# Twelve hidden blocks read back on another queue, and the products for the gates on another accumulation bank

## The chip, the cores and the metric

One core of a Trainium2 chip runs the whole kernel as one program. TensorE (PE, with PEld for its weight loads), VectorE (DVE), ScalarE (ACT), GpSimd (POOL) and SyncE (SP) each run a list of instructions in a fixed order and wait for each other through semaphores. The metric is the device time of the core in microseconds, the median of several runs.

## What is computed

The reference is one decoder layer on x of 512 tokens by 2048 channels, all in fp32. Six rows of modulation come from one vector c:

```python
mod = silu(c) @ w_ada + b_ada                      # 6 rows of 2048: sh1, sc1, g1, sh2, sc2, g2
h = rmsnorm(x, norm1_g) * (1 + sc1) + sh1
x = x + g1 * hybrid_mixer(h, ...)                  # w_in, convolution and RWKV-7 heads, w_out
h = rmsnorm(x, norm2_g) * (1 + sc2) + sh2
x = x + g2 * ((silu(h @ w_ff1) * (h @ w_ff3)) @ w_ff2)   # inner width 5632
out = rmsnorm(x, norm_f_g)
```

## The kernel before

**Products.** Each fp32 matrix is split into a high half (`hi`, a cast on ACT, L89) and a low half (`lo`, a subtraction on DVE, L90), and each product is three matmuls into one PSUM bank (`mm3`, L73): high by high, high by low, low by high. Weights come from HBM in blocks of 512 KB into tiles `ws` (four buffers) and `ws2` (six more while the first two feed-forward matrices run); their halves are `wh` and `wl` (three pairs). A unit of work is one such set of blocks; `stream` (L273) fetches two units ahead, hands their splits to ACT and DVE between matmuls, and calls a unit's `before` ahead of its first matmul. The code is written in one order; a scheduler then sets the order on each engine and queue, so that a load can stand far from where the code has it. SP's queue carries all weight loads, in its fixed order; each waits until its buffer has been read.

**w_ff1 and w_ff3.** `fast_units` (L1128) computes both products with seven instead of eight block products. It runs over 11 column blocks of 512 (c = 0 to 10); each has part 0 (four units of 12 steps, left operands `xh0` to `xh11`, `xl0` to `xl11`) and part 1 (four units of 16 steps, left operands in other tiles). A step is one `mm3`. For part 1, and the third product of part 0, DVE first takes differences of weight blocks (L1416), then the low half. The sums of a column block are turned (transposed) on PE during the next one's part 0. Of the 44 blocks of 128 hidden rows that result, the first 12 are split and written to DRAM as `hidd` (24 transfers of 256 KB), the next 28 are written unsplit as `rawd`, and the last four stay.

**Reading the 12 blocks back.** `open_hid` (L1215) is the `before` of column block 10, part 1, unit 0. It puts `hidd` back into `xh0` to `xh11` and `xl0` to `xl11`, whose old contents part 0 of that column block reads last. It issues on POOL's queue.

**w_ff2.** `ff2_units` (L1258) takes the 44 hidden blocks in three parts of 12, 16 and 16, and in each part four rows of output columns (cc = 0 to 3), each into four PSUM banks, one for each 128 tokens (t = 0 to 3). After a row's last product, DVE multiplies each bank by the gate g2 (`tm`, L910) and adds it to x. `get4` (L1221) brings four `rawd` blocks into the single buffer `hr` on POOL's queue, and `split4` splits them.

**The gates.** A lane (`ada`, L861) streams w_ada in 16 blocks of 256 KB through three buffers `wa` on SP's queue and sums them on DVE (L879). Then one fp32 product with ones (`ada_rows`, L886) spreads the sum over all partitions, and an ACT copy (L892) puts it into `rows`, which the DVE products read.

**Banks.** From the second row of w_out on, `row_acc` (L52) hands out the eight banks in a ring: the counter `nrow` moves by one with each call. `aux` (L62), which gives the gates' product its bank, calls `row_acc` too.

Of the kernel before, what the change touches and what calls it, by code (L numbers as in the profile page):

```python
# [8 lines left out]
F32 = mybir.dt.float32  # L9
# [17 lines left out]
NF = DFF // P  # L27
# [8 lines left out]
class Block:  # L36
# [24 lines left out]

    def aux(self):  # L62
        if self.rowp is not None:
            return self.row_acc()
        return self.bg.tile([P, 512], F32, name="bk", bufs=2)

    def gg(self):
# [878 lines left out]
    def run(self):  # L946
        nc, i, tc = self.nc, self.i, self.tc
# [154 lines left out]
        def make_b(kp):  # L1102

            v = nc.vector
            raw = f["raw"][kp]
            if kp % 2 == 0:
                f["yh"].append(self.xp.tile([P, NT, 512], F32R, name="x1", bufs=4)
                               .rearrange("p (k a) c -> p k (a c)", k=2))
            v.tensor_tensor(out=raw[:, 2], in0=raw[:, 2], in1=raw[:, 3], op=ALU.add)
            v.tensor_tensor(out=raw[:, 0], in0=raw[:, 2], in1=raw[:, 0], op=ALU.subtract)  # L1110
            v.tensor_tensor(out=raw[:, 1], in0=raw[:, 1], in1=raw[:, 0], op=ALU.subtract)
            f["yl"].append(self.xr.tile([P, 4, 256], F32R, name="raw", bufs=KB // 2 + 1)
                           .rearrange("p a c -> p (a c)"))
            self.split(f["yh"][kp // 2][:, kp % 2], f["yl"][kp], raw.rearrange("p a c -> p (a c)"))
# [11 lines left out]
        KS = [list(range(12)), last4 + list(range(12, 24)), list(range(24, NF - 4))]  # L1126

        def fast_units():  # L1128
            v, s = nc.vector, nc.scalar
            for c in range(NF // 4):  # L1130
# [61 lines left out]
                for part in range(2):  # L1192
                    for u in range(4):
                        def stepped(j, part=part, u=u, c=c, turn=turn, end0=end0, end1=end1):
                            if c == 0 and part == 0 and u < 3 and j in (1, 6):
                                make_a(2 * u + 2 + j // 6)
                            if c == 0 and part == 0 and u == 3 and j in (7, 9):
                                make_b(j // 9)
                            if c == 0 and part == 1 and u < 3 and j in (1, 7):
                                make_b(2 * u + 2 + j // 7)  # L1200
                            if c and part == 0 and u in (1, 2) and j in (1, 6):
                                turn(2 * (u - 1) + j // 6)
                            if u == 3:
                                (end0, end1)[part](j)
                        x = Fast(self, i["w_ff1"][0], i["w_ff3"][0], part, u, 512 * c, acc, lhs,
                                 {(0, 0, 0): open_h2, (NF // 4 - 1, 1, 0): open_hid}.get((c, part, u)), stepped)
                        if (c, part, u) == (NF // 4 - 1, 1, 3):
                            x.emit = {0: 1, 4: 1, 8: 2, 12: 2}
                        yield x
# [2 lines left out]

        hh, hl = {}, {}

        def open_hid():  # L1215
            for j, k in enumerate(KS[0]):
                hh[k], hl[k] = self.place(j)
                for n, x in enumerate((hh[k], hl[k])):
                    nc.gpsimd.dma_start(out=x.bitcast(F32), in_=self.hidd[k, n])

        def get4(k):  # L1221
            f["four"] = k, self.ff.tile([P, 4, T], F32, name="hr", bufs=1)
# [78 lines left out]
        def units():  # L1301
            yield from in_units()
            yield from out_units()
            yield from fast_units()
            yield from ff2_units()
# [173 lines left out]
```

## Time and profile before

| | us |
|---|---|
| median of 3 runs | 2521.3 |
| lowest and highest of them | 2519.9 and 2525.35 |
| the profiled execution | 2524.72 |
| its span, first to last instruction | 2523.0 |
| PE busy | 2390.0 (95%) |
| DVE busy | 1778.3 (70%) |
| ACT busy | 1049.7 (42%) |
| DMA, mean over the span | 184 GB/s |

The span is one execution; 1.7 us of its time lie outside it. An engine's busy time tells how much work it had, and its waits tell which other engine or transfer it stood still for. The granted clock of TensorE stands beside each stretch as a share of full speed: 1.00 is 2.4 GHz, 0.50 is 1.2 GHz, and a number between is a mean over both levels.

### The profile page before, as it was taken

The page shows a single profiled execution, that of the slowest core. Times are in us where ns is not written, and L with a number is a line of the kernel's source. Part 1 is how long each engine was busy: PE and PEld are TensorE (multiplying, and loading weights), DVE is VectorE, ACT ScalarE, POOL GpSimd, SP SyncE. Part 2 cuts the span into 40 slices and gives each one's busy share as a digit, 9 for nine tenths or more (in the row PEclk, how much of TensorE's full clock was granted, in tenths as well). Part 3 has the DMA queues.
Part 4 walks back from the last instruction along what each step waited for, and adds up shares of the span by engine and source line. Part 5 has one row for each costly group of instructions (what it writes and reads, how often), then busy time and mean ns, then how long its engine had stood idle before and what let it go on. Part 6 is the DMA issues. An engine that isn't in the chain of part 4 may idle for free. (4 is left out here: it accounts for less than half of the span.)

```text
span 2523.0 us, 36138 instructions
## 1 busy us (share of the span) xinstructions
PE 2390.0 (95%) x13984; PEld 1869.6 (74%) x13984; DVE 1778.3 (70%) x2726; ACT 1049.7 (42%) x1518; POOL 154.4 (6%) x256
## 2 busy tenths in 40 slices
PE   5989899999999998989999999999999999999998
PEld 4666667766766666778778878887877778788886
DVE  5664878888888885679877868777776857434434
ACT  4253364365364342255444444444444432222222
POOL 2010200110110100000000000000001000000000
PEclk9999999999999998999999999999999999999999
DMA  9953335344344448846777777776778776333322
GB/s 336 345 161 90 84 109 147 89 140 128 81 142 129 148 160 295 266 152 196 241 237 244 216 224 223 231 229 209 228 222 271 266 263 220 128 100 109 104 96 104
DMA packets 337836, 464.30 MB, mean 184 GB/s; under 512 B 42979, under 2 KB 165073, under 8 KB 336640
## 3 DMA queue, kind: packets, MB, share of 16 engines
q1 hardware_dynamic: 327856, 430.34, 54.8%
q0 software_dynamic: 9808, 31.66, 3.4%
q8 instruction: 109, 1.79, 0.3%
q14 instruction: 63, 0.52, 0.1%
HBM read 431.52 MB, written 30.41 MB: 183 GB/s over the span
## 5 line engine op out<-in xcount | busy, mean ns | idle before, releaser
L89 ACT CAST wh<-ws 128x512 fp32r<-128x512 f32 (+1 forms) x696 | 548.7, 810 | 903.3 <-PE b L71 697.0
L90 DVE TENSOR_TENSOR wl<-ws,wh 128x512 fp32r<-128x512 f32 (+1 forms) x696 | 638.6, 934 | 255.2 <-ACT wh L89 254.4
L71 PE MATMUL b<-wl,xh 128*128 128x512 f32 x1232 | 487.0, 395 | 13.4 <-DVE wl L90 13.4
L71 PE MATMUL b<-wh,xh 128*128 128x512 f32 x1232 | 490.5, 398 | 4.4 <-DVE tm L910 4.4
L71 PE MATMUL b<-wh,xl 128*128 128x512 f32 x1232 | 484.5, 394 | 0.0
L71 PEld LDWEIGHTS b<-wl,xh 128*128 128x128 f32 x1232 | 233.8, 190 | 69.9 <-DVE wl L90 21.3
L71 PE MATMUL b<-wh,x 128*128 128x512 f32 x704 | 274.6, 390 | 4.9 <-DVE xh L1140 4.8
L71 PE MATMUL b<-wl,x 128*128 128x512 f32 x704 | 274.6, 390 | 2.4 <-DVE wl L90 2.4
L71 PE MATMUL b<-wh,raw 128*128 128x512 f32 x704 | 274.3, 390 | 0.0
L71 PEld LDWEIGHTS b<-wh,xh 128*128 128x128 f32 x1232 | 233.8, 190 | 53.6 <-DVE tm L910 4.9
L71 PEld LDWEIGHTS b<-wh,xl 128*128 128x128 f32 x1232 | 233.5, 190 | 49.9 <-issue 0.8
L71 PE MATMUL acc<-xh,wh 128*128 128x512 f32 x592 | 259.3, 438 | 2.8 <-ACT wh L89 2.8
L71 PE MATMUL acc<-xl,wh 128*128 128x512 f32 x592 | 242.5, 410 | 0.0
L879 DVE SCALAR_TENSOR_TENSOR ada<-wa,sc,ada 128x512 f32<-128x512 f32 x256 | 192.7, 753 | 68.4 <-DMA wa<-in_w_ada_dram 54.4
L71 PE MATMUL acc<-xh,wl 128*128 128x512 f32 x592 | 239.5, 405 | 0.0
L1416 DVE TENSOR_TENSOR ws<-ws,ws 128x1024 f32<-128x1024 f32 x123 | 150.4, 1223 | 97.2 <-DMA ws<-in_w_ff_dram 96.4
L71 PEld LDWEIGHTS b<-wh,x 128*128 128x128 f32 x704 | 132.2, 188 | 34.1 <-issue 6.9
L71 PEld LDWEIGHTS b<-wl,x 128*128 128x128 f32 x704 | 132.2, 188 | 31.1 <-DVE wl L90 4.0
L71 PEld LDWEIGHTS b<-wh,raw 128*128 128x128 f32 x704 | 132.2, 188 | 27.3
L71 PEld LDWEIGHTS acc<-xh,wh 128*128 128x128 f32 x592 | 112.1, 189 | 35.2 <-issue 5.1
L71 PEld LDWEIGHTS acc<-xh,wl 128*128 128x128 f32 x592 | 112.7, 190 | 27.5 <-issue 2.5
L71 PEld LDWEIGHTS acc<-xl,wh 128*128 128x128 f32 x592 | 113.0, 191 | 24.4 <-issue 5.8
(375 smaller groups left out, 2906.8 us busy)
## 6 DMA issues: line engine op xcount, KB each, us to landing
ws<-in_w_ff_dram SPq DMA_DIRECT2D x440, 512.0 KB
wa<-in_w_ada_dram SPq DMA_DIRECT2D x256, 256.0 KB
ws<-in_w_in_dram SPq DMA_DIRECT2D x74, 512.0 KB
wa<-in_w_ada_dram SPq DMA_DIRECT2D x32, 1024.0 KB
ws<-in_w_out_dram SPq DMA_DIRECT2D x24, 512.0 KB
rawd<-wa POOLq DMA_DIRECT2D x28, 256.0 KB, 5.0
hr<-rawd POOLq DMA_DIRECT2D x7, 1024.0 KB, 6.6
hidd<-wa POOLq DMA_DIRECT2D x24, 256.0 KB, 4.8
```

Source lines behind the costliest of these rows:

```text
L71: return self.nc.tensor.matmul(out, lhsT=lhsT, rhs=rhs, start=start, stop=stop, skip_group_check=True)
L89: self.nc.scalar.copy(out=hi, in_=x)
L90: self.nc.vector.tensor_tensor(out=lo, in0=x, in1=hi.bitcast(F32), op=ALU.subtract)
L879: nc.vector.scalar_tensor_tensor(out=acc, in0=was[r], scalar=self.sc[:, r:r + 1], in1=acc, op0=ALU.mult, op1=ALU.add)
L1416: sub = lambda out, a, b: k.nc.vector.tensor_tensor(out=out, in0=a, in1=b, op=ALU.subtract)
```

## The change

Two edits. The first: `open_hid` is called three times, as the `before` of units 1, 2 and 3 of part 1 of column block 10, with four of the 12 blocks each time, and issues on SP's queue instead of POOL's. The second: `aux` takes bank `(nrow + 3) % 8` of the ring, which is the last of the four that the next row will take, and leaves the counter where it is. The lines of the new file stand one to three lower than those of the profile.

```diff
     def aux(self):
         if self.rowp is not None:
-            return self.row_acc()
+            return self.bank(self.banks[(self.nrow + 3) % 8])
...
                         x = Fast(self, i["w_ff1"][0], i["w_ff3"][0], part, u, 512 * c, acc, lhs,
-                                 {(0, 0, 0): open_h2, (NF // 4 - 1, 1, 0): open_hid}.get((c, part, u)), stepped)
+                                 open_h2 if (c, part, u) == (0, 0, 0) else None, stepped)
+                        if (c, part) == (NF // 4 - 1, 1) and u:
+                            x.before = lambda u=u: open_hid(u)
...
-        def open_hid():
-            for j, k in enumerate(KS[0]):
-                hh[k], hl[k] = self.place(j)
+        def open_hid(u):
+            for k in range(4 * (u - 1), 4 * u):
+                hh[k], hl[k] = self.place(k)
                 for n, x in enumerate((hh[k], hl[k])):
-                    nc.gpsimd.dma_start(out=x.bitcast(F32), in_=self.hidd[k, n])
+                    nc.sync.dma_start(out=x.bitcast(F32), in_=self.hidd[k, n])
```

Where the instructions go is told by the order on each engine, since the scheduler moves loads. The numbers behind names are buffers in the order of the program: 16618 to 16624 are the weights of part 1, unit 1 of column block 10, 16685 and up those of unit 2, 16545 to 16551 those of unit 0.

SP's queue, before, from the last two blocks that stand ahead of unit 1's weights:

```order
L1412 DMA ws2_16622<-in_w_ff3_dram 128x2x512
L1412 DMA ws_16551<-in_w_ff1_dram 128x2x512
L1412 DMA ws_16618<-in_w_ff3_dram 128x2x512
L1412 DMA ws_16620<-in_w_ff1_dram 128x2x512
L1412 DMA ws2_16624<-in_w_ff1_dram 128x2x512
L870 DMA wa_17067<-in_w_ada_dram 128x512
L870 DMA wa_17069<-in_w_ada_dram 128x512
L1412 DMA ws2_16685<-in_w_ff3_dram 128x2x512
L870 DMA wa_17084<-in_w_ada_dram 128x512
L1412 DMA ws2_16687<-in_w_ff1_dram 128x2x512
L870 DMA wa_17093<-in_w_ada_dram 128x512
L870 DMA wa_17104<-in_w_ada_dram 128x512
```

SP's queue, after, from the same block:

```order
L1415 DMA ws2_16622<-in_w_ff3_dram 128x2x512
L1415 DMA ws_16551<-in_w_ff1_dram 128x2x512
L1222 DMA xl0_16773<-hidd_68 128x512
L1222 DMA xh1_16776<-hidd_68 128x512
L1222 DMA xl1_16777<-hidd_68 128x512
L1415 DMA ws_16618<-in_w_ff3_dram 128x2x512
L1222 DMA xh2_16780<-hidd_68 128x512
L1415 DMA ws_16620<-in_w_ff1_dram 128x2x512
L1222 DMA xl2_16781<-hidd_68 128x512
L1222 DMA xh3_16784<-hidd_68 128x512
L1415 DMA ws2_16624<-in_w_ff1_dram 128x2x512
L1222 DMA xl3_16785<-hidd_68 128x512
```

Of the 24 transfers, `xh0` alone stands further up (six weight loads ahead of `xl0`); the others follow among the next eleven weight loads, five of them behind the last one of column block 10. The w_ada loads that stood among these weights come behind all of them.

POOL's queue, before, at the first of the 24 transfers (they share it with the writes of `rawd`):

```order
L1219 DMA xh0_16693<-hidd_68 128x512
L1219 DMA xl0_16694<-hidd_68 128x512
L1219 DMA xh1_16697<-hidd_68 128x512
L1219 DMA xl1_16698<-hidd_68 128x512
L1219 DMA xh8_16725<-hidd_68 128x512
L1219 DMA xl8_16726<-hidd_68 128x512
L1185 DMA rawd_69<-wa_16496 128x512
L1219 DMA xh2_16701<-hidd_68 128x512
L1219 DMA xl2_16702<-hidd_68 128x512
```

POOL's queue, after, from the write of `rawd` that stands among them above:

```order
L1186 DMA rawd_69<-wa_16496 128x512
L1186 DMA rawd_69<-wa_16523 128x512
L1186 DMA rawd_69<-wa_16569 128x512
L1186 DMA rawd_69<-wa_16596 128x512
L1226 DMA hr_17274<-rawd_69 128x4x512
L1226 DMA hr_17384<-rawd_69 128x4x512
```

Here all 24 are gone, and the writes of `rawd` and the reads of `hr` follow each other.

DVE, before, around the third product of part 0, unit 3 (`wl_16631`) and the first of part 1 (`wl_16650`):

```order
L90 TENSOR_TENSOR wl_16631<-ws2_16476,wh_16630 128x1024
L879 SCALAR_TENSOR_TENSOR ada_17064<-wa_17067,sc_96,ada_17064 128x512
L879 SCALAR_TENSOR_TENSOR ada_17064<-wa_17069,sc_96,ada_17064 128x512
L90 TENSOR_TENSOR wl_16650<-ws2_16545,wh_16649 128x1024
L1140 TENSOR_TENSOR xh12_10280<-b4_16436,xh13_10282 128x512
L1140 TENSOR_TENSOR xl12_10281<-b5_16444,xl13_10283 128x512
L90 TENSOR_TENSOR wl_16671<-ws2_16547,wh_16670 128x1024
```

DVE, after, from the same split:

```order
L91 TENSOR_TENSOR wl_16631<-ws2_16476,wh_16630 128x1024
L91 TENSOR_TENSOR wl_16650<-ws2_16545,wh_16649 128x1024
L1141 TENSOR_TENSOR xh12_10280<-b4_16436,xh13_10282 128x512
L1141 TENSOR_TENSOR xl12_10281<-b5_16444,xl13_10283 128x512
L91 TENSOR_TENSOR wl_16671<-ws2_16547,wh_16670 128x1024
L1141 TENSOR_TENSOR b0_16417<-xh13_10282,b2_16454 128x512
L1141 TENSOR_TENSOR b1_16426<-xl13_10283,b3_16462 128x512
```

The 16 sums of the first gate move down by some 19 places at their start: 15 of them now stand among the splits of units 2 and 3, the last one ahead of the first split of `hr`.

PE, before, at the seam of w_ff2's first and second part: the last matmul of row 3 (bank b0), then t = 0, 1 and 2 of the new row 0 and the first matmul of its t = 3; the last gate's product, some rows above, went to b1, and row 3 used b7, b4, b5, b0:

```order
L71 MATMUL b0_17927<-wh_18091,xl11_16738 128x512
L71 MATMUL b2_18233<-wh_18148,hl_17153 128x512
L71 MATMUL b2_18233<-wl_18149,hl_17153 128x512
L71 MATMUL b2_18233<-wh_18148,hl_17153 128x512
L71 MATMUL b3_18234<-wh_18148,hl_17153 128x512
L71 MATMUL b3_18234<-wl_18149,hl_17153 128x512
L71 MATMUL b3_18234<-wh_18148,hl_17153 128x512
L71 MATMUL b6_18235<-wh_18148,hl_17153 128x512
L71 MATMUL b6_18235<-wl_18149,hl_17153 128x512
L71 MATMUL b6_18235<-wh_18148,hl_17153 128x512
L71 MATMUL b7_18236<-wh_18148,hl_17153 128x512
```

PE, after, at the same place; the last gate's product went to b1 here too, and row 3 used b2, b3, b6, b7:

```order
L72 MATMUL b7_17927<-wh_18091,xl11_16959 128x512
L72 MATMUL b4_18233<-wh_18148,hl_17153 128x512
L72 MATMUL b4_18233<-wl_18149,hl_17153 128x512
L72 MATMUL b4_18233<-wh_18148,hl_17153 128x512
L72 MATMUL b5_18234<-wh_18148,hl_17153 128x512
L72 MATMUL b5_18234<-wl_18149,hl_17153 128x512
L72 MATMUL b5_18234<-wh_18148,hl_17153 128x512
L72 MATMUL b0_18235<-wh_18148,hl_17153 128x512
L72 MATMUL b0_18235<-wl_18149,hl_17153 128x512
L72 MATMUL b0_18235<-wh_18148,hl_17153 128x512
L72 MATMUL b1_18236<-wh_18148,hl_17153 128x512
```

The order is the same, the banks are others: t = 3 of the new row takes b7 before, which row 3 used for t = 0, and b1 after, which the last gate's product used.

## Rows read from the trace of the kernel before

**Rows 1.** Waits of PE from 1900 to 2200 us: total, times, longest.

```profile
PE b L71 <- DVE wl L90: 7.3, 4, 4.2
PE b L71 <- DVE tm L910: 3.7, 1, 3.7
PE b L1176 <- DVE hl L90: 2.2, 1, 2.2
```

**Rows 2.** Stretches: us; busy PE, PEld, DVE, ACT, POOL (instructions); granted clock; DMA share; GB/s.

```profile
1866.00:1910.00 44.00, 42.62 (x187) 34.52 (x186) 31.98 (x30) 19.03 (x21) 0.54 (x1) 1.00 0.67 200
1926.00:1970.00 44.00, 38.98 (x165) 30.88 (x164) 27.47 (x28) 17.98 (x21) 14.94 (x28) 0.92 0.94 334
1929.00:1947.00 18.00, 14.72 (x70) 11.59 (x68) 8.19 (x8) 7.38 (x9) 6.25 (x12) 0.99 1.03 383
1947.00:1960.00 13.00, 11.50 (x40) 9.03 (x40) 7.77 (x7) 4.09 (x6) 3.73 (x7) 0.75 0.82 267
1960.00:1977.00 17.00, 14.45 (x60) 11.03 (x60) 13.23 (x16) 6.89 (x8) 3.19 (x6) 1.00 0.95 342
2145.00:2165.00 20.00, 15.85 (x55) 11.81 (x55) 13.67 (x23) 4.84 (x9) 1.50 (x2) 0.83 0.38 134
```

**Rows 3.** Timeline of DVE, 1929 to 1947 us: start, us, engine, line, operation, idle before.

```profile
1929.72 1.23 DVE L90 TENSOR_TENSOR wl<-ws,wh 128x1024 fp32r<-128x1024 f32 x1
1935.05 1.22 DVE L1416 TENSOR_TENSOR ws<-ws,ws 128x1024 f32<-128x1024 f32 x1 [4.10 <-DMA ws<-in_w_ff_dram]
...
1944.21 2.48 DVE L1416 TENSOR_TENSOR ws<-ws,ws 128x1024 f32<-128x1024 f32 x2 [5.67 <-DMA ws<-in_w_ff_dram]
1946.62 1.22 DVE L90 TENSOR_TENSOR wl<-ws,wh 128x1024 fp32r<-128x1024 f32 x1
```

**Rows 4.** The DMAs that read hidd, 1900 to 2000 us: count, issue times, us to landing.

```profile
L1219 POOL DMA_DIRECT2D xh<-hidd x12: 536/536/541, 1926.9 to 1965.8; - x12
...
DMA to landing us min/median/max: 2.9/6.0/8.1
```

**Rows 5.** DMA issues from 1926 to 1970 us: queue, kind, packets, MB, share of 16 engines.

```profile
q1 hardware_dynamic: 4098, 7.84, 52.2%
q0 software_dynamic: 2079, 6.84, 41.4%
```

**Rows 6.** Waits of PE from 1620 to 1920 us, the four column blocks ahead.

```profile
PE b L71 <- DVE wl L90: 2.5, 5, 1.1
PE b L71 <- DVE xh L1140: 2.5, 2, 1.3
```

**Rows 7.** Timeline of ACT at the seam of parts one and two of w_ff2.

```profile
2156.01 1.66 ACT L89 CAST xh<-hr 128x512 fp32r<-128x512 f32 x3 [8.49 <-DMA hr<-rawd]
2157.57 0.57 ACT L892 COPY rows<-b 128x512 f32<-128x512 f32 x1
```

**Rows 8.** Timeline of DVE at the same seam.

```profile
2145.82 0.68 DVE L90 TENSOR_TENSOR xl<-hr,xh 128x512 fp32r<-128x512 f32 x1
...
2148.69 0.74 DVE L879 SCALAR_TENSOR_TENSOR ada<-wa,sc,ada 128x512 f32<-128x512 f32 x1
...
2156.66 1.90 DVE L90 TENSOR_TENSOR xl<-hr,xh 128x512 fp32r<-128x512 f32 x3 [5.41 <-ACT xh L89]
2158.47 1.28 DVE L910 TENSOR_TENSOR tm<-b,rows 128x512 f32<-128x512 f32 x2
```

**Rows 9.** Timeline of POOL, 2000 to 2165 us.

```profile
2012.92 0.77 POOL L1223 DMA_DIRECT2D hr<-rawd  x1 [46.08 <-DMA ws<-in_w_ff_dram]
...
2149.38 0.76 POOL L1223 DMA_DIRECT2D hr<-rawd  x1 [16.51 <-DVE wl L90]
```

**Rows 10.** Timeline of SP's queue, 2000 to 2031 us.

```profile
2012.65 0.34 SPq L1255 DMA_DIRECT2D x<-x1d  x1
...
2017.42 0.58 SPq L1255 DMA_DIRECT2D x<-x1d  x1
```

**Rows 11.** The DMA into hr issued at 2012.9 us, and the next: us to landing.

```profile
DMA to landing us min/median/max: 10.2/10.3/10.4
```

## The prediction

> **What bounds the kernel now.** PE is busy 95% of the span, so only time in which PE stands still or runs at the lower clock can be won. I read first the list of whom PE waits for, in the stretch that the change touches (1900 to 2200 us). It has, beside one of 0.4 us, three kinds of waits for 13.2 us together: four for the low half of a weight block, 7.3 us, the longest 4.2; one of 3.7 us for `tm`; one of 2.2 us for the last hidden blocks [rows 1]. Then I read the stretches. Around the first four PE is idle and then runs slow: 14.72 us busy of 18 in 1929 to 1947, 11.50 of 13 at a mean clock of 0.75 in 1947 to 1960, 14.45 of 17 in 1960 to 1977. The DMA engines are full there: share 1.03 at 383 GB/s, then 0.82 and 0.95. Over 1926 to 1970 they move 334 GB/s, where the same place of the column block ahead (1866 to 1910) has 200 at a share of 0.67 and PE busy 42.62 of 44 us [rows 2]. DVE's timeline shows how a full DMA reaches PE. DVE stands 4.10 us and then 5.67 us in front of the differences of L1416, waiting for weight blocks of part 1, and the split that PE needs for part 0 starts behind them at 1946.62 [rows 3]. PE's wait of 4.2 us ends with that split. So DVE's fixed order makes a late load for later work a stall of present work. What fills the DMA engines is plain: in 1926 to 1970 POOL's queue moves 6.84 MB beside 7.84 MB on SP's, with 41.4% and 52.2% of the engines' time [rows 5]. The 24 reads of `hidd`, 12 into `xh` and 12 into `xl`, are issued there, from 1926.9 us on, as each buffer falls free [rows 4], though PE uses them only in w_ff2, well after 2000 us.
>
> **The change part by part.** *The reads move to SP's queue.* POOL loses 24 issues of 536 ns, 12.9 us; nobody waits for POOL there but the writes of `rawd`, which stood between the reads. On SP each read costs an issue of about 0.34 us, as other loads do [rows 10], 8.2 us in all. SP stands waiting for free buffers most of the time, and that covers it; where up to three reads stand ahead of a weight load, that load goes at most 1.0 us later, which is in the remainder below. Would SP's queue be blocked, since a read waits until PE has let go of its buffer? Before, the first was free at 1926.9 us and all 24 by about 1966 [rows 4]. In SP's new order only `xh0` stands early; the next comes behind six more weight loads, the last five behind all weights of the column block. The nearest case is `xh6`, whose buffer is read in part 0, unit 3; the weights behind it belong to part 1, unit 2, one unit later. I take nothing for it.
>
> What is won is the stall. While DVE stood at its two differences, POOL's reads took nearly half of the engines; in the new order one read of 0.26 MB is in front of those loads. The four waits are 7.3 us [rows 1]. The lower clock that follows them costs 11.50 us times 0.25, 2.9 us [rows 2]. Together 10.2 us.
>
> What remains of it? At the least what other column blocks have: in the four ahead PE waits 2.5 + 2.5 = 5.0 us for the same engines, 1.25 each [rows 6]. At the most all 10.2, if the weights come as late as before. To choose, I count bytes. A unit of part 1 is 48 matmuls of 42.62 us / 187 = 0.228 us, 10.9 us. Eleven weight loads of 0.524 MB and the 19 reads that stand ahead of the last weights (5.0 MB) make 10.8 MB in three units, 32.8 us: 329 GB/s, under the 383 that the engines have shown [rows 2]. So the queue gets through, with little room, and a weight load may stand behind up to three reads, 0.79 MB, or 2.1 us. With three pairs of `wh` and `wl` the splits run up to two blocks, 5.4 us, ahead of PE. That is nearer to the lower end: I take 2.0 us.
>
> *The first gate's sums.* 16 sums on DVE move behind the differences and start with unit 2. Between two splits stand at most two of them, 2 x 0.74 us [rows 8] beside a split of 1.23 us [rows 3], 2.7 us; PE needs a split each 12 matmuls, 2.7 us. DVE's lead covers this; without it, some 0.1 us a pair, 0.8 us, stays within the range. The gate is used after w_ff2's first row, over 30 us later.
>
> *The bank at the seam.* In w_ff2's first part the rows now alternate between two sets of four banks, so t = 3 of a new row no longer waits for `tm` on t = 0 of the row before. At the first three seams PE shows no wait. At the fourth it waits 3.7 us [rows 1] until `tm` has read b7. `tm` came late because DVE stood 5.41 us for a cast of `hr`, whose transfer landed at 2156.0. `tm` on b7 is the first of the two at 2158.47, done at 2159.15 [rows 8]. After, t = 3 is on b1, where the gate's product stood, and waits for ACT's copy of it. But that copy stands behind three casts of the same `hr`, at 2157.57 for 0.57 us, to 2158.14 [rows 7]. So the wait ends 1.0 us earlier and no more; the hold is the transfer, not the bank. The lower clock there (15.85 us at 0.83, 2.7 us [rows 2]) I leave in place; its bounds are 0 and 2.7 of gain. I take 1.0. At the other seams and at w_out's rows nine matmuls (t = 0 to 2), 2.1 us, and the tail of the row before stand between the product and its bank's next use, and the copy of 0.57 us fits in; without them that copy would be the wait. I take nothing.
>
> *`hr` and `x1d`.* In the new order the second load of `x1d` (1 MB) stands one weight block after the first and no longer waits to 2017.42 [rows 10]. So it competes longer with the first `hr` transfer, issued at 2012.92 [rows 9], which took 10.4 us [rows 11] and set PE's wait of 2.2 us. At worst the whole 1.05 MB goes first, 2.7 us at 383 GB/s; at best nothing changes, as the engines were nearly full anyway. Half a microsecond of loss, nearer the lower end.
>
> **The sum.** -10.2 + 2.0 - 1.0 + 0.5 = -8.7 us. The profiled execution took 2524.7 us and would take 2516.0. It stands 3.4 us above the median of the three runs, 2521.3; the same step from the median gives **2512.6 us**.
>
> **The rivals.** *A: the stall only moves.* The same bytes run on the same DMA engines in nearly the same stretch, and a weight load that stands behind reads in its own queue is as late as one that shares with POOL's. For it speaks the share of 0.95 to 1.03 [rows 2]; against it that the five last reads and the 15 w_ada loads leave the stretch. Then all 10.2 us stay: -1.0 + 0.5 = -0.5, 2520.8 us. The Trainium skill, "DMA: Bandwidth & Descriptors", section "Issuing engines are not separate DMA queues", says that DMAs started by the scalar, sync or gpsimd engine run on the same 16 engines and interleave, so that the starter makes no difference; by that alone the time would be this rival's. The trace agrees that the two queues fill one pool; it does not show a case where one of them is moved.
>
> *B: SP's queue becomes the bound, and it is slower.* In units 1 to 3 of part 1, reads (2.1 MB a unit) stand in one line with weights (2.1 MB). At 383 GB/s a unit's 4.2 MB take 11.0 us, PE's pace; at the 267 GB/s of 1947 to 1960 [rows 2] they take 15.7, 4.8 us late in each of three units, and each stall brings a spell of lower clock of 2.9 us: 23.1 us in place of 10.2, net +12.4 with the other terms, 2533.7 us. It decides from about 318 GB/s down (13.2 us a unit: 6.9 + 8.7 = 15.6 us, 5 us over today's). Against it: the rate of 267 was that of a stretch where DVE kept SP waiting, not that of full engines.
>
> *C: the seam opens wholly.* The `hr` transfer at the seam was issued at 2149.38 [rows 9], 2.9 us after the last reader of the buffer had ended (2146.5 [rows 8]). If that delay is absent once timing has shifted, the data come as much earlier and PE's 3.7 us with their 2.7 us of clock vanish, 5.4 us beyond my 1.0: 2507.2 us.
>
> **How the numbers follow.** A run of this kernel is told from no change at about 0.2%, 5 us: faster is below 2516.3, slower above 2526.3. The forecast (2508 to 2516) has 0.58, C 0.09, A with what lies around it 0.23, B 0.10. Faster is 0.58 + 0.09 = 0.67, same 0.23, slower 0.10. The range goes from just below C, 2506.5, to 2519.5, which leaves out B and about half of A.
>
> **What would show it.** Right: between part 0, unit 2 and part 1, unit 1 of the last column block PE's waits for low halves fall from 7.3 to about 2 us, with no stretch at half clock; DVE's waits at L1416 fall below 4 us each; POOL's queue carries a few `rawd` writes there and no reads; the DMA share stays around 0.9, longer. At the seam PE waits about 2.7 us, for ACT's copy. Wrong: if PE waits in part 1, units 1 to 3, as long as it did in part 0, A or B holds, and the length of a unit against 10.9 us tells which. If the seam has no wait at all, C. If the waits are gone and the time is not, I have mistaken what they cost.

## The result, and the profile after

The changed kernel takes 2510.2 us (median of four runs, 2508.1 to 2512.1), the kernel before 2523.3 us in its four: a ratio of 0.9939, 95% interval 0.9916 to 0.9962. The profiled execution has a span of 2509.4 us, against 2523.0 before.

The list of whom PE waits for, 1900 to 2200 us, after (total, times, longest):

```profile
PE b L72 <- DVE wl L91: 3.4, 1, 3.4
PE b L1177 <- DVE hl L91: 1.8, 1, 1.8
```

Of the four waits for low halves [rows 1] one is left, at 1958.95 us. The wait for `tm` at the seam of w_ff2's first and second part is gone altogether. The stretches that answer to [rows 2] (us; busy PE, PEld, DVE, ACT, POOL with instructions; clock; DMA share; GB/s):

```profile
1926.00:1970.00 44.00, 40.61 (x187) 33.06 (x186) 33.19 (x33) 20.71 (x25) 2.17 (x4) 1.00 0.89 299
1945.00:1960.00 15.00, 11.61 (x54) 9.05 (x53) 9.75 (x10) 6.46 (x8) 1.08 (x2) 1.00 0.88 308
1960.00:1977.00 17.00, 17.00 (x77) 14.07 (x76) 14.91 (x16) 7.57 (x8) 0.00 (x0) 1.00 1.01 357
...
2139.00:2159.00 20.00, 19.98 (x85) 15.44 (x84) 15.07 (x25) 7.15 (x13) 1.50 (x2) 1.00 0.51 173
```

In 1926 to 1970 PE runs 187 matmuls where it ran 165, at full clock throughout; the DMA engines move 299 GB/s instead of 334. In 1960 to 1977 they stand at a share of 1.01, and PE is busy all of it: full DMA engines alone do not hold PE up there. The last row lies around the seam: 85 matmuls in 20 us at clock 1.00, where [rows 2] had 55 at 0.83.

The one wait left has the form of those before. DVE's timeline, 1928 to 1965 us (start, us, engine, line, operation, idle before):

```profile
1936.40 1.23 DVE L1419 TENSOR_TENSOR ws<-ws,ws 128x1024 f32<-128x1024 f32 x1 [2.46 <-DMA ws<-in_w_ff_dram]
...
1942.95 2.49 DVE L1419 TENSOR_TENSOR ws<-ws,ws 128x1024 f32<-128x1024 f32 x2 [3.06 <-DMA ws<-in_w_ff_dram]
...
1947.95 2.35 DVE L91 TENSOR_TENSOR wl<-ws,wh 128x1024 fp32r<-128x1024 f32 x2
1955.28 1.22 DVE L1419 TENSOR_TENSOR ws<-ws 128x1024 f32<-128x1024 f32 x1 [4.97 <-DMA ws<-in_w_ff_dram]
1956.54 1.22 DVE L1419 TENSOR_TENSOR ws<-ws,ws 128x1024 f32<-128x1024 f32 x1
1957.68 1.22 DVE L91 TENSOR_TENSOR wl<-ws,wh 128x1024 fp32r<-128x1024 f32 x1
```

In front of the two differences at which DVE stood 4.10 and 5.67 us before [rows 3], it now stands 2.46 and 3.06 us. In front of a later one, for part 1, unit 1, it stands 4.97 us, and the split that PE needs now stands behind two of them and ends at 1958.9.

**A measure with less noise.** PE runs the same 13,984 matmuls in the same order in every kernel of this study, so the time from the start of one of them to the start of another can be compared. Five of them divide the rest of the program: the first of part 1 of column block 9 (1878.9 us before), the first turning of the last hidden blocks that waited (2027.7), the last gate's product ahead of the seam (2149.5), a matmul of the second part's first row (2169.6), and the last of all (2511.3). Stretch A runs from part 1 of column block 9 over the last column block to the last hidden blocks, PE's wait for them included; B is w_ff2's first part, C the seam, D the rest. All in us, from one profiled execution each; ratios from all runs, against runs of the kernel before on the same chip:

| kernel | start of A | A | B | C | D | A to D | ratio (95%) |
|---|---|---|---|---|---|---|---|
| before | 1878.9 | 148.8 | 121.7 | 20.1 | 341.6 | 632.3 | 1 |
| after | 1881.8 | 141.0 | 119.6 | 13.8 | 341.6 | 616.0 | 0.9939 (0.9916 to 0.9962) |
| e1_alone | 1874.3 | 142.8 | 120.0 | 14.8 | 341.6 | 619.2 | 0.9944 (0.9925 to 0.9963) |
| e2_alone | 1879.4 | 150.0 | 119.5 | 20.6 | 341.6 | 631.6 | 0.9979 (0.9964 to 0.9995) |
| sp_unit0 | 1871.2 | 139.8 | 119.7 | 14.9 | 341.6 | 616.0 | 0.9915 (0.9889 to 0.9941) |
| pool_units | 1879.8 | 147.0 | 120.5 | 20.7 | 341.6 | 629.8 | 0.9986 (0.9972 to 0.9999) |
| no_reads | 1882.9 | 139.4 | 120.1 | 13.9 | 341.6 | 615.0 | 0.9942 (0.9924 to 0.9960) |
| hold_u2 | 1883.2 | 140.2 | 122.0 | 13.5 | 341.6 | 617.3 | 0.9955 (0.9943 to 0.9967) |
| hold_u3 | 1889.0 | 139.5 | 121.5 | 13.6 | 341.6 | 616.1 | 0.9953 (0.9940 to 0.9966) |
| x1_late | 1883.6 | 142.2 | 121.8 | 13.5 | 341.6 | 619.1 | 0.9950 (0.9928 to 0.9972) |
| after_dup24 | 1895.8 | 139.5 | 119.5 | 20.4 | 341.6 | 621.0 | 1.0006 (0.9987 to 1.0025) |
| before_pad | 1897.7 | 152.5 | 122.9 | 20.2 | 348.4 | 643.9 | 1.0106 (1.0093 to 1.0119) |
| before_pad16 | 1893.1 | 153.1 | 122.9 | 20.2 | 347.1 | 643.3 | 1.0092 (1.0065 to 1.0119) |
| after_pad | 1895.6 | 142.2 | 122.7 | 14.0 | 348.4 | 627.3 | 1.0051 (1.0038 to 1.0064) |

The start of A differs by up to 18 us (1871 to 1889) among the first ten kernels, though all that they change ahead of it is the bank of a few gates' products, in some of them; that scatter of single executions goes into the ratios too. How far a ratio can be trusted shows in pool_units: its instructions stand in the order of the kernel before on every engine and queue, and its interval (0.9972 to 0.9999) still leaves out 1; so 0.2% alone, as of e2_alone, shows nothing. From A on, the change gives 632.3 - 616.0 = 16.3 us: 7.8 in A, 2.1 in B, 6.4 in C (rounded).

### The profile page after: what moved, and what is told of

Its sections match the earlier page's. It is cut to its first block, busy times and chain, and to the rows that moved or that the text cites. A ratio compares the mean times of both kernels' runs of the same rounds, so it can differ in the third digit from the quotient of the medians.

```text
span 2509.4 us, 36134 instructions
## 1 busy us (share of the span) xinstructions
PE 2387.5 (95%) x13984; PEld 1868.2 (74%) x13984; DVE 1779.0 (71%) x2726; ACT 1051.9 (42%) x1518; POOL 142.2 (6%) x232
## 5 line engine op out<-in xcount | busy, mean ns | idle before, releaser
L72 PEld LDWEIGHTS b<-wh,xl 128*128 128x128 f32 x1232 | 232.0, 188 | 49.2 <-issue 0.5
```

Source lines behind the costliest of these rows:

```text
L72: return self.nc.tensor.matmul(out, lhsT=lhsT, rhs=rhs, start=start, stop=stop, skip_group_check=True)
```

## The experiments

**The two halves.** e1_alone is the changed kernel with the old `aux`, e2_alone the kernel before with the new one.

```diff
 # e1_alone, against after
     def aux(self):
-            return self.bank(self.banks[(self.nrow + 3) % 8])
+            return self.row_acc()
 # e2_alone, against before: the same lines the other way round
```

Expected of e1_alone:

> The first edit alone: the 24 reads as in the changed kernel, the gates' products on the old banks. Theory Q (the gain of the first edit comes from the reads' place in SP's queue): between part 0, unit 2 of the last column block and the last hidden blocks PE gains 9 to 10 us on the kernel before, with one wait of about 3.4 us left for a low half; 2512 to 2514 us. Theory B (the second edit opened the seam of w_ff2's parts one and two): here the seam then keeps PE's wait of 3.7 us for tm and its spell at half clock. Theory L (the seam opened since POOL issued the transfer into hr 0.3 us after the buffer's last reader in place of 2.9 us, by chance or by the shifted timing): hr is issued promptly, tm ends about 1 us after PE arrives, PE waits 0.8 to 1.3 us there; 2509 to 2512 us.

Expected of e2_alone:

> The second edit alone: the reads on POOL's queue as before, the gates' products on the last of the next four banks. Both theories: the four waits for low halves from 1940 to 1980 us, 7.3 us with their half clock, stay. Theory B: the seam has no wait, 3.7 us and 2.4 to 3.4 us of half clock are gone, 2515 to 2517 us. Theory L: if hr is issued late again, PE waits about 2.7 us for ACT's copy in place of 3.7, 2521 to 2523 us; if hr is issued promptly, the seam is open here as well and opens in kernels with the old banks to within 1.3 us.

The longest of PE's waits, 1900 to 2200 us, in e1_alone:

```profile
PE b L1177 <- DVE hl L91: 2.9, 1, 2.9
PE b L72 <- DVE wl L91: 2.8, 2, 2.4
PE b L72 <- DVE tm L911: 1.1, 1, 1.1
```

and in e2_alone:

```profile
PE b L71 <- DVE wl L90: 10.5, 4, 7.1
PE b L71 <- ACT rows L892: 4.6, 1, 4.6
PE b L1176 <- DVE hl L90: 1.4, 1, 1.4
```

The first edit does most of it, 13.1 of the 16.3 us from A on, at the seam too: theory L, not B. Its gain in A is 6.0 us (5.7 from part 0, unit 2 on), less than the 9 to 10 expected: it has one long wait left (2.4 us), and 3.4 us at half clock behind that. With the old banks the seam keeps a wait of 1.1 us for `tm` and no half clock. With the new banks alone the seam stays shut for 4.6 us; only the engine in the list has changed, from DVE's `tm` to ACT's copy. POOL's timeline in e2_alone and in e1_alone, the two `hr` transfers around the seam:

```profile
2132.20 0.75 POOL L1223 DMA_DIRECT2D hr<-rawd  x1 [15.28 <-DVE xl L90]
2148.94 0.76 POOL L1223 DMA_DIRECT2D hr<-rawd  x1 [15.99 <-DVE wl L90]
```

```profile
2119.94 0.75 POOL L1226 DMA_DIRECT2D hr<-rawd  x1 [15.26 <-DVE xl L91]
2134.90 0.75 POOL L1226 DMA_DIRECT2D hr<-rawd  x1 [14.21 <-DVE xl L91]
```

and the splits that read the buffer last ahead of the second one, from DVE's timelines of the same two:

```profile
2145.38 0.68 DVE L90 TENSOR_TENSOR xl<-hr,xh 128x512 fp32r<-128x512 f32 x1
```

```profile
2133.92 0.69 DVE L91 TENSOR_TENSOR xl<-hr,xh 128x512 fp32r<-128x512 f32 x1
```

In e2_alone the transfer goes out at 2148.94, 2.88 us after the reader's end (2146.06); in e1_alone at 2134.90, 0.29 us after it (2134.61). The list names `wl` as releaser in the first, but that one's end lies at no fixed distance: in the six kernels with a late issue, the last of DVE's instructions to end ahead of it did so 0.02 to 0.6 us before, while `xl`, the buffer's last reader, always ended 2.88 us before. The kernel before shows 2.88 as well (2146.50 to 2149.38, [rows 8, 9]). So this is no chance of one execution. The changed kernel itself is prompt, 0.29 us behind its last reader; the reader and the transfer, from the timelines of DVE and POOL:

```profile
2139.28 0.69 DVE L91 TENSOR_TENSOR xl<-hr,xh 128x512 fp32r<-128x512 f32 x1
```

```profile
2140.26 0.75 POOL L1226 DMA_DIRECT2D hr<-rawd  x1 [14.13 <-DVE xl L91]
```

**Queue or calls.** Does the first edit work by the queue or by the three later calls?

```diff
 # sp_unit0, against before: still one call, ahead of unit 0
-                    nc.gpsimd.dma_start(out=x.bitcast(F32), in_=self.hidd[k, n])
+                    nc.sync.dma_start(out=x.bitcast(F32), in_=self.hidd[k, n])
 # pool_units, against after, and with the old aux: three calls
-                    nc.sync.dma_start(out=x.bitcast(F32), in_=self.hidd[k, n])
+                    nc.gpsimd.dma_start(out=x.bitcast(F32), in_=self.hidd[k, n])
```

Expected of sp_unit0:

> The kernel before with one change: the 24 reads are issued on SP's queue in place of POOL's, still by one call ahead of part 1, unit 0; old banks. The scheduler spreads them among the weight loads nearly as in the changed kernel; only the last four weight loads stand behind all reads. Theory Q: the same 9 to 10 us are gained up to the last hidden blocks, less what the last four weights lose by standing behind eight more reads (2.1 MB, at most 5.5 us at 383 GB/s); 2510 to 2517 us. Theory T (the gain comes from issuing them in three later units): no gain, 2521 to 2525 us.

Expected of pool_units:

> The kernel before with one change: the reads are issued by three calls ahead of units 1, 2 and 3 of part 1, four blocks each, but on POOL's queue; old banks. Theory T: the waits of 7.3 us go as in the changed kernel, 2512 to 2516 us. Theory Q: POOL has nothing else to do and issues each read when its buffer falls free, at the same times as before, so all stays: four waits of about 7 us, 2521 to 2525 us. For theory L it is one more look at when hr is issued with before's timing: 2.9 us after the last reader if the delay belongs to that timing, 0.3 us if it was chance.

The longest of PE's waits, 1900 to 2200 us, in sp_unit0 and in pool_units:

```profile
PE b L1176 <- DVE hl L90: 2.3, 1, 2.3
PE b L71 <- DVE wl L90: 2.0, 1, 2.0
PE b L71 <- DVE tm L910: 1.1, 1, 1.1
```

```profile
PE b L72 <- DVE wl L91: 6.7, 3, 3.5
PE b L72 <- DVE tm L911: 4.2, 1, 4.2
PE b L1177 <- DVE hl L91: 1.1, 1, 1.1
```

It is the queue. Three calls on POOL's queue leave A at 147.0 us; one call on SP's brings it to 139.8. The scheduler lays the three calls' reads exactly where the one call's lay, so pool_units is another execution of the order of the kernel before, and its 147.0 against 148.8 shows how far one order scatters in A. POOL issues each read when its buffer falls free, wherever the call stands. Its row for these reads in pool_units (count, duration, first and last issue) reads as [rows 4] do:

```profile
L1222 POOL DMA_DIRECT2D xh<-hidd x12: 536/536/541, 1927.7 to 1969.0; - x12
```

On SP's queue the scheduler lays the same reads between the weights nearly as in the changed kernel, from one call too. sp_unit0 has the lowest ratio of all, but from A on it takes 616.0 us as the changed kernel does; its lead in the profile lies ahead of A, in work that it doesn't touch, so I don't put it down to the edit.

DVE's two stands of 4.10 and 5.67 us [rows 3] show the same in all kernels: 3.3 to 5.4 and 5.7 to 9.3 us in the five with these reads on POOL's queue, 1.4 to 2.5 and 1.1 to 3.2 us in the nine with them on SP's or without them. The second in pool_units:

```profile
1944.09 2.48 DVE L1419 TENSOR_TENSOR ws<-ws,ws 128x1024 f32<-128x1024 f32 x2 [5.80 <-DMA ws<-in_w_ff_dram]
```

**What is left of the reads' cost.** no_reads leaves the reads out, so that w_ff2's first part multiplies what the buffers held before; hold_u2 and hold_u3 keep the reads back. The stretch of 148.8 and 141.0 us in the first expectation is A, which begins earlier than it says, at part 1 of column block 9.

```diff
 # no_reads, against before
-                hh[k], hl[k] = self.place(j)
-                for n, x in enumerate((hh[k], hl[k])):
-                    nc.gpsimd.dma_start(out=x.bitcast(F32), in_=self.hidd[k, n])
+                hh[k], hl[k] = f["x"][j]
 # hold_u2, hold_u3, against after; fast_held: the last weight load of part 1, unit 2 or 3
...
-                    nc.sync.dma_start(out=x.bitcast(F32), in_=self.hidd[k, n])
+                    with tc.issue_after(self.fast_held):
+                        nc.sync.dma_start(out=x.bitcast(F32), in_=self.hidd[k, n])
```

Expected of no_reads:

> The kernel before without the 24 reads: w_ff2's first part multiplies with what the buffers held before, so that the reads' whole cost shows. Theory Q: column block 10 then has the waits of the other column blocks, at most 1.3 us each, and the stretch from its first matmul of part 0, unit 1 to the last hidden blocks, 148.8 us before and 141.0 us after the change, takes 137 to 139 us; so the changed kernel still pays 2 to 4 us for the reads. If the waits came from something else than the reads, they stay. POOL's queue has carried 24 transfers less, so by theory V the transfer into hr at the seam is issued promptly here too.

Expected of hold_u2:

> The changed kernel with one thing more: all 24 reads are held behind the last weight load of part 1, unit 2 in SP's queue (an order of issue, no wait). Theory Q says the weights that DVE's differences wait for then come without a read ahead of them: the wait of 3.4 us for a low half that the changed kernel still has near 1959 us falls to 1.3 us or less. The reads are issued from about 1965 us and 6.3 MB need 16.4 us at 383 GB/s, so they land some 30 us ahead of their first use. 2 to 4 us faster than the changed kernel, 2506 to 2508 us. If instead full DMA engines make the wait, wherever the reads stand, a wait of 2 to 4 us appears one or two units later, and the time stays 2508 to 2512 us.

Expected of hold_u3:

> As the one before, but the reads are held behind the last weight load of column block 10 (part 1, unit 3). Theory Q: no wait over 1.3 us for a low half in this column block, 2506 to 2508 us. Against it: the reads, issued from about 1975 us, then compete with the first weights of w_ff2 and w_ada, and the first row of w_ff2 or the first gate could wait for them: up to 3 us there, 2508 to 2512 us.

The longest of PE's waits, 1900 to 2200 us, in no_reads and in hold_u2:

```profile
PE b L71 <- DVE wl L90: 2.4, 1, 2.4
PE b L1176 <- DVE hl L90: 0.9, 1, 0.9
PE b L71 <- DVE xh L1140: 0.8, 1, 0.8
```

```profile
PE b L1177 <- DVE hl L91: 2.6, 1, 2.6
PE b L72 <- DVE wl L91: 1.4, 1, 1.4
PE b L72 <- DVE xh L1141: 0.8, 1, 0.8
```

Without any read A takes 139.4 us, 9.4 us less than before (148.8) and 1.6 us less than after (141.0). The 9.4 us stand clear of the scatter; the 1.6 do not. With the reads on SP's queue A takes 139.5 to 142.8 us in five executions that hold nothing back (after, e1_alone, sp_unit0, x1_late, after_dup24), and 0.9 of the 1.6 us is a shorter wait for the last hidden blocks (0.9 against 1.8). So what the reads still cost is somewhere from 0 to 3 us. A wait of 2.4 us for a low half stays without them, where I had expected at most 1.3. DVE's timeline in no_reads, at the differences that the changed kernel shows at 1936.40, 1942.95 and 1955.28:

```profile
1936.67 1.22 DVE L1414 TENSOR_TENSOR ws<-ws,ws 128x1024 f32<-128x1024 f32 x1 [2.10 <-DMA ws<-in_w_ff_dram]
...
1942.94 2.48 DVE L1414 TENSOR_TENSOR ws<-ws,ws 128x1024 f32<-128x1024 f32 x2 [2.63 <-DMA ws<-in_w_ff_dram]
...
1954.65 1.23 DVE L1414 TENSOR_TENSOR ws<-ws 128x1024 f32<-128x1024 f32 x1 [4.68 <-DMA ws<-in_w_ff_dram]
```

The last stand is there without any read, 4.68 us against 4.97, and in every kernel of the table (2.4 to 5.5 us; 3.6 before). So most of the wait left at 1959 is not the reads'; what it comes from is open. A rival for the gain in A is that the first edit also moves the w_ada loads out of this stretch. It falls: no_reads issues six of them in 1926 to 1970 us, the kernel before five, and A is short all the same.

Held back, the reads are issued from 1966.2 us (hold_u2) and 1981.5 us (hold_u3) on, the wait falls to 1.4 us in hold_u2 and is gone in hold_u3, and A is 140.2 and 139.5, the way theory Q said, though after_dup24 has 139.5 with nothing held. PE's waits for the last hidden blocks, which lie in A, are 2.6 and 2.8 us, and behind them it runs at half clock for 3.4 us in both, in B: 122.0 and 121.5 against 119.6. The kernel before has such a spell there too (B 121.7), so the hold is not shown to be its cause. From A on both take as long as the changed kernel or longer, so the forecast of 2 to 4 us missed.

**The first transfer into `hr`.** It takes 10 us, and DVE stands still for it ahead of the last hidden blocks.

```diff
 # x1_late, against after; held: a w_ff2 weight load that went out at 2015.84 us
...
-            nc.sync.dma_start(out=xt, in_=self.x1d[t * P:(t + 1) * P])
+            with tc.issue_after(f["held"]):
+                nc.sync.dma_start(out=xt, in_=self.x1d[t * P:(t + 1) * P])
```

Expected of it:

> The changed kernel with one thing more: the four loads of x1d (1 MB each) are held in SP's queue behind a w_ff2 weight load that went out at 2015.84 us in the changed kernel; there the first two went out at 2009.07 and 2012.63, beside the first transfer into hr (2008.28 to 2018.35, 10.1 us), for which DVE stands still ahead of the last hidden blocks. If hr is late since x1d shares the DMA engines with it, hr lands after 4 to 6 us, DVE is through its splits sooner, PE's wait of 1.8 us for the last hidden blocks goes, and the spell at half clock that follows it in some executions (1.7 us) too: 1.5 to 3.5 us faster than the changed kernel. If hr is late for its own size or since the weights fill the engines, it still takes 8 us or more and nothing moves; if x1d then comes too late for the first row's sums, PE waits at 2045 us and it is slower.

`hr` was issued at 2011.3, the first load of `x1d` at 2018.9, and ACT's first cast of `hr` began at 2021.4: 10.0 us, as with `x1d` beside it from 2009.1 us on (10.1). The wait for the last hidden blocks stays (1.9 us), and the list has two waits for sums of w_ada, 1.8 us together, that the changed kernel's has not. So `x1d` is not what holds `hr` up; what does is open.

**Why POOL is late at the seam.** Four kernels bear on the delay of 2.88 us. The first three add small POOL memsets in the code ahead of column block 0; the fourth adds transfers to POOL's queue.

```diff
 # before_pad (8), after_pad (48); before_pad16: 8, with [P, 16]
+            spare = self.const.tile([P, 1], F32, name="spare", bufs=1)
+            for _ in range(8):
+                nc.gpsimd.memset(spare, 0.0)
 # after_dup24, against after; dupd: a place in DRAM that nobody reads
...
                         nc.gpsimd.dma_start(out=self.hidd[k, n], in_=x)
+                        nc.gpsimd.dma_start(out=self.dupd[k, n], in_=x)
```

Expected of before_pad:

> The kernel before with eight small POOL memsets (128 by 1, into a tile that nobody reads) added ahead of the first column block; every other instruction stands in the same order on every engine. In all three kernels so far whose reads stand on POOL's queue (442 POOL instructions in the trace) POOL issues the transfer into hr for w_ff2's second part 2.88 us after the buffer's last reader, in all three whose reads stand on SP's (395) 0.29 us. Theory P (the delay sits at a fixed place in POOL's instruction list, which that transfer happens to occupy): eight instructions more move the place to a memset that nobody waits for, hr is issued after 0.3 us, PE's wait at the seam falls from 3.7 to 0.8 to 1.3 us and the spell at half clock goes; 4 to 6 us faster than before, 2517 to 2520 us. Theory V (it comes from the amount of work on POOL's DMA queue, or from timing): the delay stays 2.88 us, and so does the time, 2521 to 2525 us. The four waits near 1940 to 1980 us stay in both.

Expected of after_pad:

> The changed kernel with 48 small POOL memsets added ahead of the first column block, so that the transfer into hr for w_ff2's second part has the same place in POOL's instruction list as in the kernel before. Nothing else is moved. Theory P: the delay of 2.88 us comes back, hr lands 2.6 us later, PE waits some 2.5 to 3 us at the seam with a spell at half clock; 4 to 6 us slower than the changed kernel, 2514 to 2517 us. Theory V: the issue comes 0.3 us after the last reader, no wait, 2508 to 2512 us.

Expected of after_dup24:

> The changed kernel with 24 more transfers on POOL's queue: each write of the first 12 hidden blocks is issued twice, the second time to a place that nobody reads, in column blocks 1 to 3. So the transfer into hr for w_ff2's second part is again the 114th of 116 on POOL's queue, as in the kernel before, in place of the 90th of 92; nothing else moves near it. Theory V (the delay of 2.88 us after the buffer's last reader goes with the number of transfers that POOL's queue has carried): it comes back, hr lands 2.6 us later, and PE waits 2 to 3 us at the seam with a spell at half clock. Theory W (it needs the reads of the hidden blocks at that place, or the timing of the kernel before): hr is issued 0.3 us after its last reader, and the seam stays at 13.5 to 13.8 us. The writes themselves may cost up to 3 us in column blocks 1 to 3.

Expected of before_pad16:

> The kernel with eight more POOL memsets once more, with one difference: the tile that they write is 16 elements (64 bytes) a partition in place of one (4 bytes). With 4 bytes the matmuls became slower by 2 to 3% from column block 0 on (1 us for some 165 matmuls), 26 us in all, though no engine's order moved; the tile stands ahead of the operands in SBUF and shifts all of them. Theory A (the matmuls read operands slower whose addresses are shifted by 4 bytes): with 64 bytes they are as fast as before, 2520 to 2527 us. Theory M (the memsets or their place in the program cost it): 2548 to 2555 us again. The delay of hr stays 2.88 us in both.

DVE's last reader of `hr` in before_pad, after_pad and after_dup24, and POOL's issue behind it, from the timelines of the two engines:

```profile
2169.02 0.68 DVE L90 TENSOR_TENSOR xl<-hr,xh 128x512 fp32r<-128x512 f32 x1
```

```profile
2172.58 0.76 POOL L1226 DMA_DIRECT2D hr<-rawd  x1 [16.43 <-DVE wl L90]
```

```profile
2157.43 0.69 DVE L91 TENSOR_TENSOR xl<-hr,xh 128x512 fp32r<-128x512 f32 x1
```

```profile
2158.41 0.75 POOL L1229 DMA_DIRECT2D hr<-rawd  x1 [14.68 <-DVE xl L91]
```

```profile
2151.74 0.68 DVE L91 TENSOR_TENSOR xl<-hr,xh 128x512 fp32r<-128x512 f32 x1
```

```profile
2155.30 0.76 POOL L1228 DMA_DIRECT2D hr<-rawd  x1 [16.45 <-DVE ada L880]
```

The delays are 2.88, 0.29 and 2.88 us. Theory P falls twice: eight more instructions don't move the delay away, and the old place in the instruction list doesn't bring it back. Theory V stands: 24 more transfers bring it back in the changed kernel, the seam takes 20.4 us again, and PE waits 4.6 us there for ACT's copy:

```profile
PE b L72 <- ACT rows L893: 4.6, 1, 4.6
```

In all kernels of the table it is one or the other: 2.88 us in the six where `hr` is the 114th of 116 transfers on POOL's queue, 0.3 us in the eight where it is the 90th of 92. The transfers just ahead of it and behind it go out after 0.3 us in both. no_reads, which has the reads on neither queue, is prompt as well, as expected of it. Whether it goes by the number of transfers, their bytes or their descriptors was not told apart.

after_dup24 starts A 14 us later than the changed kernel, where 3 us had been allowed for its writes; how much of that is scatter is not known. The pads cost 11 to 12 us from A on and 14 to 19 ahead of it, which I had not expected; that is below.

## Why the prediction was right, and where it was not

- **The stall of DVE (-10.2).** Right in mechanism and size. The waits are gone but for one, and so is the half clock (in e1_alone and x1_late one spell of 3.4 us came). A is 7.8 us shorter where the step with its remainder gave 8.2; e1_alone and sp_unit0 gained 6.0 and 9.0. That the reads on POOL's queue made the stall is shown by no_reads, and that the queue decides by pool_units and sp_unit0. The reason given, that those reads take engine time from the weights that DVE waits for, fits DVE's shorter stands; when a weight block landed no trace shows. One reading was off and changes no term: the stand of 4.10 us is in front of the third product of part 0, unit 3, not of part 1; that of 5.67 us is part 1's.
- **What remains (+2.0).** The sum with the step above came out (7.8 against 8.2 us), but the term itself is not measured closer than 0 to 3 us, and the form was wrong. I expected small delays; it came as one wait of 3.4 us, and DVE stood 4.97 us at one difference, more than the 4 us I allowed. By no_reads (2.4 and 4.68 us) most of that has other causes than the reads.
- **`hr` and `x1d` (+0.5).** Wrong sign and no effect. The first `hr` took 10.1 us after 10.4, and x1_late shows that `x1d` doesn't matter to it. The 2.1 us that B gained are mostly the spell of half clock behind PE's wait there: the kernel before had one (0.79 in 2024 to 2032), the changed one none; but e2_alone and pool_units, which leave this place alone, have none either (B 119.5 and 120.5). So I count it as luck, 2.6 us of it against the forecast's loss of 0.5.
- **The bank (-1.0).** The size was right where the data are prompt: C is 14.8 and 14.9 us with old banks and reads on SP's queue, 13.5 to 13.8 with new banks. In no_reads, with old banks, `hr` took some 0.5 us less and C is 13.9, so the gain is 0 to 1.4. Where `hr` is late C is 20.1 to 20.7 with either bank; with the new banks PE waits for ACT's copy behind the casts of `hr`, as the step said it would, though for 4.6 us where it gave 2.7. `hr` took 8.2 and 7.9 us to land there with the new banks (e2_alone, after_dup24), 6.6 and 7.4 us with the old (before, pool_units), so a gain of 1 us may be hidden.
- **The step that failed: the seam's transfer taken as given.** C fell by 6.4 us where the sum had 1.0. The working saw that `hr` went out 2.9 us after its last reader, put it into rival C with 5.4 us, and gave that 0.09. The 5.4 us are what came: 1.0 + 5.4 = 6.4. What failed is that I held the delay for one of timing; it belongs to POOL's queue, and the edit takes 24 transfers off that queue. With it the sum is -14.1 us, and 2521.3 - 14.1 = 2507.2; measured is 2510.2, within the scatter ahead of A.
- **How near the number came.** 2512.6 stands 2.4 us from 2510.2, and part of that is luck: the forecast step was -8.7 us, the measured one -13.1 between the medians and -16.3 from A on in the traces, and the median of the kernel before rose by 2.0 us with a fourth run.
- **Rival A and the page.** The time went the way of the forecast, not the way that the prediction drew from the Trainium skill's rule in "DMA: Bandwidth & Descriptors", section "Issuing engines are not separate DMA queues". The runs don't contradict that the engines are one pool; pool_units moves 8.02 and 6.37 MB on the two queues in 1926 to 1970 us, about as before. They show that the starter still matters, by what stands in front of what in its order: A is 147.0 to 150.0 with POOL, 139.5 to 142.8 with SP (the pads, whose matmuls are slower, left aside).
- **Rival B.** In units 1 to 3 no wait came; each unit took 10.9 us from its first matmul to the next unit's, the length named in the prediction. At 357 GB/s and a share of 1.01 (1960 to 1977 us) PE was busy all the time.

## What to carry to other kernels

When a bulk transfer competes with loads that an in-order engine waits for, try it in the same queue behind those loads; here its own queue let it in as soon as its buffer was free, wherever the code called it. When an edit takes transfers off a queue, look at that queue's later issues too: each issue's distance from the event that frees it is read from two rows, and a long one is a cost that the edit may move. Where single executions scatter by some tenths of a per cent, compare the same instruction's start in both traces, stretch by stretch, before a total is believed; and look whether the scheduler has changed the order at all, as it had not in pool_units.

## What was not expected of the hardware

**One late issue on POOL's queue.** It comes at a fixed transfer, 2.6 us later than its neighbours, in all six kernels with 116 transfers on that queue, and in none of the eight with 92. What POOL does in that time no trace shows.

**Operands' places in SBUF and the rate of the matmuls.** before_pad adds a tile of 4 bytes a partition, before_pad16 one of 64 bytes; no engine's order changes but for POOL's eight memsets. In the built programs `xh`, `xl`, `hr`, `hl` and `hid` then lie 32 and 64 bytes further up, while `wh`, `wl` and the weight buffers stay; so the shift was 32 bytes where the expectation has 4. The stretch 2200 to 2400 us, deep in w_ff2, in before, before_pad and before_pad16:

```profile
2200.00:2400.00 200.00, 200.00 (x875) 164.30 (x874) 79.22 (x126) 48.16 (x88) 0.75 (x1) 1.00 0.31 102
```

```profile
2200.00:2400.00 200.00, 200.00 (x858) 160.96 (x857) 71.17 (x112) 45.67 (x80) 0.75 (x1) 1.00 0.31 98
```

```profile
2200.00:2400.00 200.00, 200.00 (x862) 161.64 (x861) 71.23 (x112) 45.57 (x80) 0.75 (x1) 1.00 0.31 100
```

PE is busy all of it at full clock in all three, at 200 us / 875 = 228.6 ns a matmul, then 233.1 and 232.0. Theory A in the form "as fast as before with 64 bytes" falls, and the time is the one that theory M named (2550.6 us). In before_pad the scheduler put the memsets at 19.3 to 20.4 us, 0.1 us each, so their own time doesn't explain it; whether their place in the program does was not tried, by a tile without memsets or memsets into a tile that is there already. That the operands lie elsewhere is the likelier cause, but it is argued and not shown; which addresses are good was not tried. For the study of the delay the pads still serve, since POOL's issue is measured against its own reader.

**The clock after a wait.** PE's wait of 3.4 us at 1959 is followed by clock 1.00 (1960 to 1977); the wait of 3.7 us at the seam before, by a mean of 0.83 in 2145 to 2165 [rows 2]; and in e1_alone one of 2.4 us near 1950 by a spell of 3.4 us at half clock, in x1_late one of 3.2 us near 1960 by another. One wait's length does not tell which.
